# Up-projection over experts that a token block uses: count, scatter to sorted rows, gather

## The chip, the cores and the metric

One core of one Trainium2 chip. The metric is device time in microseconds of one execution, the median of several runs. TensorE (PE) multiplies matrices, VectorE (DVE), ScalarE (ACT) and GpSimd (POOL) work elementwise, and SP issues most of the DMAs.

## The reference, cut to what matters

Three transformer layers run on 256 tokens of width 1024. The last stage of the last layer is a mixture of 16,384 experts, each of which is one row of `peer_down` and one row of `peer_up`:

```python
q = (hblk @ w_q).reshape(B, TB, PEER_HEADS, 2, PEER_DHALF)
s = jnp.einsum('btphd,phnd->btphn', q, subkeys)
v, i = lax.top_k(s, PEER_TOPK)
...
tv, tj = lax.top_k(cand, PEER_TOPK)
eidx = jnp.take_along_axis(cidx, tj, axis=-1)
w = jax.nn.softmax(tv, axis=-1)
u = w_down[eidx]
a = jax.nn.gelu(jnp.einsum('btd,btpkd->btpk', hblk, u))
vv = w_up[eidx]
return jnp.einsum('btpk,btpkd->btd', (w * a), vv)
```

Each token picks 16 experts in each of 8 heads, 128 in all, by the sum of two key scores: expert = 128 x first key + second key. The result is scaled by `ga2`, added to the residual and normalised.

## The kernel before, in words

The kernel does not gather. It computes the down product of all 16,384 experts with all 256 tokens, multiplies it by a gate that is zero where a token has not picked an expert, and multiplies the result with all of the up matrix. An expert block `e` is 256 experts, two tiles `a` of 128; there are `NE` = 64 blocks. Tokens lie in two blocks `tt` of 128. Every fp32 operand is split in a high and a low part (`put_hl`, line 363; `load`, line 298: ScalarE casts `wh`, VectorE subtracts `wl`), and `mm3` (line 358) makes three matmuls of each product.

In the **gate stage** (`with tc.tile_pool(name="rp")`, lines 1457 to 1640) scores and top-16 give each token's picks. `gen_chunk` (line 1574) makes one-hot matrices `L` (first key) and `R` (second key) for 8 tokens at a time and, for each token, three matmuls `Lw x R` (line 1593): a 128 x 128 gate matrix a token. Sixteen chunks of 16 tokens go to the DRAM tensor `Gd` (line 1597). The same stage fills TensorE's gaps with the down products of the first `NST` = 28 blocks (`fill`, line 1437, with a number of steps written out by hand). TensorE runs in program order; the other engines' order is fixed by hand only while `dve.on` is set.

Then two more down blocks follow (`more_down`, line 1449: 48 matmuls in a bank `mt` and a gelu into a block `A`, one of 24 buffers and six spare ones), and then the **up stage** (lines 1655 to 1677), a loop over all 64 blocks. Every fourth block loads `G`, the gates of eight tiles (line 1659, three buffers). From block 29 on each step first does one more down block. Then the gated product is made in `pt` (line 1666), split in `ph` and `pl`, 1 MB of `up` is loaded and split, and `up` (line 1651) adds to the four accumulators `upb`, one for each token block and half of the 1024 columns. A step has 2 x 2 x 2 x 3 = 24 matmuls of 512 columns:

```python
    for e in range(NE):
        if e % 4 == 0:
            ...
        if nxt[0] < NE and nxt[0] <= e + 1:
            more_down()
        ...
        u = load(I["up"][e], 2048, 1024)
```

The last block's 24 matmuls are held back and done accumulator by accumulator beside the final normalisation (lines 1679 to 1699). Weight loads go through four 1 MB buffers `wr`, and their split parts through four `wh` and four `wl` of 1024 columns. SP issues the loads in program order; a load whose buffer is still in use holds those behind it.

Of the kernel before, what the change touches and what calls it, by code (L numbers as in the profile page):

```python
# [7 lines left out]

F32 = mybir.dt.float32
F32R = mybir.dt.float32r  # L10
BF = mybir.dt.bfloat16
U32 = mybir.dt.uint32
AF = mybir.ActivationFunctionType
ALU = mybir.AluOpType
AX = mybir.AxisListType
# [2 lines left out]

NEG = -1e30
TAIL = 8  # L20
ROOT2 = 4.0 ** 0.25
D = 1024
DFF = 2816
# [115 lines left out]
def prep(z):  # L139
    o = {}  # L140
# [65 lines left out]
    o["up"] = np.ascontiguousarray(z["peer_up_2"][0].reshape(64, 2, 128, 1024).transpose(0, 2, 1, 3).reshape(64, 128, 2048))  # L206

    vec = np.zeros((128, NVEC), np.float32)

# [38 lines left out]
def build(tc, nc, I, out, dbg=None):  # L248
# [15 lines left out]
    def acc():  # L264
        return ps.tile([P, 512], F32, tag="acc", name=nm("acc"))
# [86 lines left out]
    def mm(o, l, r, start, stop):  # L352
        pe.matmul(o, l, r, start=start, stop=stop)
# [1045 lines left out]

    pp = es.enter_context(tc.tile_pool(name="pp", bufs=1))  # L1400
    NE, NA = 64, 24
    store = {}
    nxt = [0]
    spare = []
# [52 lines left out]
    with tc.tile_pool(name="rp", bufs=1) as rp:  # L1457
# [116 lines left out]
        def gen_chunk(ch):  # L1574
            stg = rp.tile([P, P, 16], F32, tag="stg", name=nm("stg"), bufs=2)
            for q8 in range(2):
                t = (ch % 8) * 16 + q8 * 8
                L = L2[:, q8]
                R = rp.tile([P, 8, P], BF, tag="R", name=nm("R"), bufs=2)
                for i, o in ((0, L), (1, R)):  # L1580
                    dve.tensor_tensor(o.rearrange("p t (n d) -> p t n d", d=4),
                                      iota1.rearrange("p (n d) -> p n d", d=4)[:, None].to_broadcast([P, 8, 32, 4]),
                                      slotb[:, i, t:t + 8][:, :, None, :].to_broadcast([P, 8, 32, 4]), op=ALU.is_equal)
                for q4 in range(2):
                    q = slice(4 * q4, 4 * q4 + 4)
                    Lw = rp.tile([P, 4, 3, P], BF, tag="Lw", name=nm("Lw"), bufs=2)
                    dve.tensor_mul(Lw.rearrange("p t j (n d) -> p t j n d", d=4),
                                   L[:, q].rearrange("p t (n d) -> p t n d", d=4)[:, :, None].to_broadcast([P, 4, 3, 32, 4]),
                                   slotp[:, t + 4 * q4:t + 4 * q4 + 4][:, :, :, None, :].to_broadcast([P, 4, 3, 32, 4]))
                    m = mt()  # L1590
                    for i in range(4):
                        for j in range(3):
                            mm(m[:, tsl(i)], R[:, 4 * q4 + i], Lw[:, i, j], start=j == 0, stop=j == 2)
                    o = 8 * q8 + 4 * q4
# [25 lines left out]
        for tt in range(2):  # L1620
            if tt == 0:
                top16(pair_rows(0, 7))
            else:
                for h in range(0, 8, 2):
                    top16(pair_rows(1, h, 2))
                    fill(10, dve, 1)
                spare.extend(xp.tile([P, 2, 512], F32, tag="row", name="Arow", bufs=2)[:, i] for i in range(2))
# [5 lines left out]
            slots_T(tt, ev)  # L1633
            fill(10, dve, 1)
# [7 lines left out]
    dve.on = False  # L1642
    for _ in range(2):
        more_down()
    mp_ = es.enter_context(tc.tile_pool(name="mp", bufs=2))

    upb = [[acc(), acc()], [acc(), acc()]]
    G = None
    gfin = row("gfin")

    def up(e, ph, pl, u, a, tt, half):
        mm3(upb[tt][half], ph[:, a, tsl(tt)], pl[:, a, tsl(tt)], u[a][0][:, csl(half)], u[a][1][:, csl(half)],
            e == 0 and a == 0, e == NE - 1 and a == 1)

    for e in range(NE):
        if e % 4 == 0:
            G = mp_.tile([P, 16, 8, 16], F32, tag="sg", name=nm("G"), bufs=3)
            c0 = 16 if e else 14
            nc.sync.dma_start(G[:, :c0], Gd[:c0, :, 2 * e:2 * e + 8, :].rearrange("c p e t -> p c e t"))
        if nxt[0] < NE and nxt[0] <= e + 1:  # L1660
            more_down()
        A = store.pop(e)
        pt = mp_.tile([P, 2, 256], F32, tag="pt", name=nm("pt"))
        for a in range(2):
            for c in ((slice(0, 16),) if e >= 4 else (slice(0, 14), slice(14, 16))):
                dve.tensor_mul(pt[:, a].rearrange("p (c t) -> p c t", c=16)[:, c],
                               A[:, a * 256:(a + 1) * 256].rearrange("p (c t) -> p c t", c=16)[:, c],
                               Gl[:, :, (2 * e + a) % 8] if c.start else G[:, c, (2 * e + a) % 8])
        ph = mp_.tile([P, 2, 256], F32R, tag="ph", name=nm("ph"))
        pl = mp_.tile([P, 2, 256], F32R, tag="pl", name=nm("pl"))  # L1670
        put_hl(ph, pl, pt)
        u = load(I["up"][e], 2048, 1024)
        if e < NE - 1:
            for a in range(2):
                for tt in range(2):
                    for half in range(2):
                        up(e, ph, pl, u, a, tt, half)

    act_set(3)
    xf, xg = new_x(), new_x()  # L1680
    for tt in range(2):
        for half in range(2):
            for a in range(2):
                up(e, ph, pl, u, a, tt, half)
# [30 lines left out]
```

## Time and profile before

| | us |
|---|---|
| median of 3 runs | 1740.83 |
| lowest to highest | 1740.42 to 1741.88 |
| the profiled execution | 1742.32 |
| its span in the trace | 1740.5 |
| TensorE busy | 1682.9 |
| VectorE busy | 1192.7 |
| ScalarE busy | 871.5 |
| GpSimd busy | 96.9 |

Times in a trace start at 0 with its span. Matmuls are pipelined and their ends are modelled, so the distance from start to start tells more than the duration shown. "DMA share" is the mean busy share of the core's 16 DMA engines. A row `out<-in` names the tile written and those read; the line shown for most instructions is that of a helper (337), so tiles tell them apart. The gate stage runs from some 990 to 1165 us, the up stage from 1177 us to the end.

### The profile page before, as it was taken

The numbers are of one execution on the slowest core, as the hardware profiler recorded it, in microseconds if no ns is written. First come the engines' busy times: TensorE is split into PE (matmuls) and PEld (weight loads), VectorE is DVE, ScalarE is ACT, GpSimd is POOL, SyncE is SP. The second block draws the span as 40 slices with busy tenths as digits, with TensorE's granted clock in tenths as the row PEclk, the third lists the DMA queues.
The fourth block names the chain that finished last, engine by engine and source line by source line (L and its number), as shares of the span: only waits on it lengthen the run. The fifth ranks groups of instructions, "written<-read, shape, count | busy, mean of one in ns | idle before, by whom it ended". The sixth has DMA issues, their size and how long they took to land.

```text
span 1740.5 us, 28199 instructions
## 1 busy us (share of the span) xinstructions
PE 1682.9 (97%) x11374; PEld 1503.1 (86%) x11374; DVE 1192.7 (69%) x2111; ACT 871.5 (50%) x1324; POOL 96.9 (6%) x74
## 2 busy tenths in 40 slices
PE   8999999999999999889999999999999999999998
PEld 7879998788889987677789999897888999999996
DVE  5659775566688755657669999986666555555555
ACT  7545444365554444654554555554444444444444
POOL 0001000100010001111037000000000000000000
PEclk9999999999999999999999999999999999999999
DMA  8427775453468764462344465577676556656551
GB/s 315 159 73 275 272 294 187 159 205 102 157 222 319 276 218 155 173 239 98 116 167 160 162 244 210 198 269 262 236 254 217 203 209 218 208 205 215 192 177 68
DMA packets 83954, 352.01 MB, mean 202 GB/s; under 512 B 6352, under 2 KB 39504, under 8 KB 46704
## 3 DMA queue, kind: packets, MB, share of 16 engines
q1 hardware_dynamic: 83024, 349.62, 56.7%
q8 instruction: 89, 1.46, 0.3%
q10 hardware_dynamic: 288, 0.52, 0.1%
q14 instruction: 41, 0.34, 0.1%
q0 software_dynamic: 512, 0.07, 0.0%
HBM read 332.30 MB, written 17.83 MB: 201 GB/s over the span
## 4 chain that ended last, share of the span: by engine, by line
PE 87%; DVE 7%; ACT 3%; DMA 1%; issue 1%; POOL 1%; SPq 0%; DVEq 0%; ACTq 0%
PE acc L337 70%; PE mt L337 17%; DVE wl L337 2%; DVE x L337 2%; ACT wh L337 1%; ACT L337 0%; POOL x L337 0%; DMA G<-Gd 0%; DVE Lw L337 0%; DVE st L337 0%; ACT P L337 0%; DMA Gd<-stg 0%; ACT x L337 0%; DMA row<-rows 0%; DMA xt<-x_T 0%
## 5 line engine op out<-in xcount | busy, mean ns | idle before, releaser
L337 DVE TENSOR_TENSOR wl<-wr,wh 128x1024 fp32r<-128x1024 f32 (+2 forms) x504 | 606.6, 1209 | 357.2 <-ACT wh L337 355.6
L337 ACT CAST wh<-wr 128x1024 fp32r<-128x1024 f32 (+3 forms) x524 | 540.5, 1034 | 551.9 <-PE acc L337 372.8
L337 PE MATMUL acc<-xh,wh 128*128 128x256 f32 x1472 | 421.7, 286 | 0.5 <-ACT xh L337 0.5
L337 PE MATMUL acc<-xl,wh 128*128 128x256 f32 x1472 | 414.1, 281 | 0.1
L337 PE MATMUL acc<-xh,wl 128*128 128x256 f32 x1472 | 414.1, 281 | 0.0
L337 PEld LDWEIGHTS acc<-xh,wh 128*128 128x128 f32 x1472 | 278.6, 189 | 2.3 <-issue 1.2
L337 PEld LDWEIGHTS acc<-xl,wh 128*128 128x128 f32 x1472 | 279.0, 190 | 0.3 <-DVE xl L337 0.3
L337 PEld LDWEIGHTS acc<-xh,wl 128*128 128x128 f32 x1472 | 278.3, 189 | 0.0
L337 PE MATMUL acc<-wh,pl 128*128 128x512 f32 x512 | 204.9, 400 | 0.5 <-DVE pl L337 0.5
L337 PE MATMUL acc<-wh,ph 128*128 128x512 f32 x512 | 201.6, 394 | 2.0 <-ACT ph L337 2.0
L337 PE MATMUL acc<-wl,ph 128*128 128x512 f32 x512 | 202.0, 395 | 0.0
L337 PE MATMUL mt<-xh,wl 128*128 128x256 f32 x576 | 161.9, 281 | 0.0
L337 PE MATMUL mt<-xl,wh 128*128 128x256 f32 x576 | 161.8, 281 | 0.0
L337 PE MATMUL mt<-xh,wh 128*128 128x256 f32 x576 | 161.8, 281 | 0.0
L337 PE MATMUL acc<-wh,xh 128*128 128x512 f32 (+5 forms) x368 | 143.7, 390 | 15.2 <-ACT wh L337 7.2
L337 PE MATMUL acc<-wh,xl 128*128 128x512 f32 (+5 forms) x368 | 140.2, 381 | 3.3 <-DVE xl L337 3.3
L337 PE MATMUL acc<-wl,xh 128*128 128x512 f32 (+5 forms) x368 | 140.5, 382 | 1.2 <-DVE wl L337 1.2
L337 PEld LDWEIGHTS acc<-wl,ph 128*128 128x128 f32 x512 | 96.6, 189 | 23.6
L337 PEld LDWEIGHTS acc<-wh,ph 128*128 128x128 f32 x512 | 96.7, 189 | 23.4 <-ACT ph L337 2.2
L337 PEld LDWEIGHTS acc<-wh,pl 128*128 128x128 f32 x512 | 96.5, 188 | 23.2 <-DVE pl L337 1.0
L337 PEld LDWEIGHTS mt<-xl,wh 128*128 128x128 f32 x576 | 108.6, 189 | 1.4
L337 PEld LDWEIGHTS mt<-xh,wh 128*128 128x128 f32 x576 | 108.5, 188 | 1.5
(290 smaller groups left out, 2252.6 us busy)
## 6 DMA issues: line engine op xcount, KB each, us to landing
wr<-f SPq DMA_DIRECT2D x64, 1024.0 KB, 5.8
wr<-dn SPq DMA_DIRECT2D x64, 1024.0 KB, 4.9
wr<-up SPq DMA_DIRECT2D x64, 1024.0 KB, 5.0
wr<-ada SPq DMA_DIRECT2D x24, 1024.0 KB, 6.6
Gd<-stg SPq DMA_DIRECT2D x16, 1024.0 KB, 4.7
G<-Gd SPq DMA_DIRECT2D x15, 1024.0 KB, 7.8
wr<-m_g SPq DMA_DIRECT2D x10, 1024.0 KB, 5.0
row<-rows SPq DMA_DIRECT2D x16, 512.0 KB, 4.5
```

The source lines that it names most:

```text
L337: inst = f(*args, **kw)
```

## The change

The up matrix is given as plain rows (`up` of 16384 x 1024) instead of packed blocks. The first 16 blocks (`NS`, 32 tiles, 4096 experts) stay as they are and are called static. For the other `NJ` = 96 tiles:

1. `gen_chunk` adds one matmul a token, `R x L` without a weight, into one accumulator bank held for the whole stage: how often each of the 12,288 experts is picked, for each token block.
2. Between two down blocks the counts become four classes (block 0 only, both, block 1 only, none), and small matmuls with a triangular matrix give each expert a position `posi` in that order. A flag is set if a class boundary breaks the constants `T0`, `T1`, `T2`.
3. All remaining down blocks are done before the first gathered row is used. `weigh` multiplies a block by its gates: static blocks in place, the others into `pt`, with the expert's own index beside the product, and GpSimd scatters 128 rows of 264 numbers to the DRAM tensor `Pd` at `posi`. One static up block comes before every fourth down block, nine in all.
4. After three more static up blocks, `row_up` reads sorted tiles of `Pd`, GpSimd gathers the 128 rows of `up` whose indices lie in them, and only those (tile, token block) pairs are multiplied that the constants allow. Fully used pairs of tiles and half-used ones alternate.
5. Behind them, every engine reads the flag, and a conditional block would do all other pairs. Then the last static block and the normalisation follow; `gfin` is loaded there.

```diff
+NS = 16
+NJ = 128 - 2 * NS
+T0, T1, T2 = 61, 20, 83
...
+                        mm(cnt_b[0][:, ch // 8 * NJ:(ch // 8 + 1) * NJ], R[:, 4 * q4 + i], L[:, 4 * q4 + i, 2 * NS:],
+                           start=n == 0, stop=n == 127)
...
-    for _ in range(2):
+    more_down()
...
+    W = 264
+    Pd = nc.dram_tensor("Pd", (NJ * P, W), F32, kind="Internal").ap()
+    Pv = dram_disjoint_views(Pd, NJ)
...
+    for c in range(4):
+        mm(b[:NJ, tsl(c)], M[:, c], oneb, start=c == 0, stop=c == 3)
+    act.copy(wk[:NJ, 192:448].bitcast(BF), b[:NJ])
+    more_down()
+    b = mt()
+    mm(b[:, :4 * NJ], tri, wk[:, 0:192].bitcast(BF), start=True, stop=False)
+    for c in range(4):
+        o = b[:, c * NJ:(c + 1) * NJ]
+        mm(o, totb[:, c], tri[:NJ, :NJ], start=False, stop=False)
+        for c_ in range(c):
+            mm(o, totb[:, c_], oneb[:NJ, :NJ], start=False, stop=False)
+        mm(b[:, 4 * NJ + c:4 * NJ + c + 1], totb[:, c], oneb[:NJ, 0:1], start=False, stop=c == 3)
...
+    for i, (n, op) in enumerate(((T1, ALU.is_lt), (T0, ALU.is_gt), (T2, ALU.is_gt))):
+        dve.tensor_scalar(few[:, i:i + 1], few[:, i:i + 1], 128.0 * n, None, op0=op)
...
+                G = mp_.tile([P, 16, 8, 16], F32, tag="sg", name=nm("G"), bufs=2)
...
+    def weigh(e):
+
+        G, A = gates(e), store[e]
+        if e < NS:
+            for a in range(2):
+                for c in ((slice(0, 16),) if e >= 4 else (slice(0, 14), slice(14, 16))):
+                    o = A[:, a * 256:(a + 1) * 256].rearrange("p (c t) -> p c t", c=16)[:, c]
+                    dve.tensor_mul(o, o, Gl[:, :, (2 * e + a) % 8] if c.start else G[:, c, (2 * e + a) % 8])
+            return
+        pt = mp_.tile([P, 2, W + 8], F32, tag="pt", name=nm("pt"), bufs=5)
+        for a in range(2):
+            i = 2 * e + a
+            pool_.iota(pt[:, a, 128:136].bitcast(I32), pattern=[[0, 8]], base=i * P, channel_multiplier=1)
...
+        for a in range(2):
+            j = 2 * (e - NS) + a
+            nc.gpsimd.indirect_dma_start(Pv[j], bass.IndirectOffsetOnAxis(ap=posi[:, j:j + 1], axis=0), pt[:, a, 0:W], None)
+        store.pop(e)
...
+    def row_parts(i, used):
+
+        tts = set(used[0]) | set(used[1])
+        tiles = [a for a in range(2) if used[a]]
+        o, n = (0, W) if len(tts) == 2 else (128 * min(tts), 136)
+        Pc = mp_.tile([P, 2, W + 8], F32, tag="pt", name=nm("Pc"), bufs=5)
...
+        for a in tiles:
+            nc.gpsimd.indirect_dma_start(r[:, a * 1024:(a + 1) * 1024], None, I["up"],
+                                         bass.IndirectOffsetOnAxis(ap=Pc[:, a, 128:129].bitcast(U32), axis=0))
...
+    for g in (0, 4, 5, 6, 1, 7, 8, 2, 9, 3, 10, 11, 12, 13, 14, 15):
+        work.extend(range(4 * g, 4 * g + 4))
...
+    su = 0
+    weigh_some(5)
+    while nxt[0] < NE:
+        if (nxt[0] - 30) % 4 == 0:
+            static_up(su)
+            su += 1
         more_down()
...
+        weigh_some(2)
+    nxt[0] += 1
+    weigh_some(len(work))
+
+    def blocks_of(j):
+        return [tt for tt, t in ((0, j < T0), (1, T1 <= j < T2)) if t]
...
+    lead = 3
+    for _ in range(lead):
+        static_up(rest.pop(0))
+    gap = len(seq) // (len(rest) + 1)
+    for n, q in enumerate(seq):
+        row_up(*q)
+        if rest and n % gap == gap - 1:
+            static_up(rest.pop(0))
...
+    v = nc.values_load(flag[0:1, 0:1])
...
+    with tc.If(v > 0, preferred_fallthrough_block=False):
...
+        for i, used in out_of:
+            ph_, pl_, u_ = row_parts(i, used)
...
     gfin = row("gfin")
```

## Rows read from the trace of the kernel before

**Rows 1.** The page: busy time by engine; GpSimd in the 40 slices.

```profile
PE 1682.9 (97%) x11374; PEld 1503.1 (86%) x11374; DVE 1192.7 (69%) x2111; ACT 871.5 (50%) x1324; POOL 96.9 (6%) x74
...
POOL 0001000100010001111037000000000000000000
```

**Rows 2.** Windows: stretch, length, busy (count) of the engines, PEclk, DMA share, GB/s.

```profile
1200.00:1300.00 100.00, 100.00 (x431) 80.42 (x430) 68.03 (x89) 46.94 (x54) 0.00 (x0) 1.00 0.69 240
1600.00:1700.00 100.00, 100.00 (x643) 90.55 (x642) 54.49 (x61) 46.29 (x54) 0.00 (x0) 1.00 0.53 189
```

**Rows 3.** Chain of waits: start, us, engine, tile, count; one pattern to 1720 us.

```profile
1348.06 5.59 PE acc L337 x24
1353.65 5.70 PE mt L337 x48
```

**Rows 4.** Windows as in rows 2, of two more stretches.

```profile
1342.00:1478.00 136.00, 136.00 (x869) 122.94 (x868) 74.09 (x84) 62.60 (x73) 0.00 (x0) 1.00 0.61 212
510.00:520.00 10.00, 10.00 (x87) 10.00 (x86) 8.77 (x11) 5.24 (x9) 0.00 (x0) 1.00 0.98 360
```

**Rows 5.** Groups of 1180 to 1718 us: count, busy us, mean ns, idle.

```profile
L337 DVE TENSOR_TENSOR wl<-wr,wh 128x1024 fp32r<-128x1024 f32 x190 | 232.8, 1225 | 197.0 <-ACT wh L337 197.0
L337 ACT CAST wh<-wr 128x1024 fp32r<-128x1024 f32 x191 | 200.6, 1050 | 248.3 <-PE acc L337 127.3 <-PE mt L337 116.1 <-issue 5.0
...
L337 DVE TENSOR_TENSOR pl<-pt,ph 128x512 fp32r<-128x512 f32 x61 | 42.0, 689 | 26.9 <-ACT ph L337 26.9
L337 DVE TENSOR_TENSOR pt<-A,G 128x256 f32<-128x256 f32 x106 | 41.8, 420 | 0.7
...
L337 ACT ACTIVATE A<-mt 128x512 f32<-128x512 f32 x33 | 19.6, 594 | 0.0
```

**Rows 6.** Groups of GpSimd, whole span, columns as in rows 5.

```profile
L337 POOL DMA_DIRECT2D qk<-dqk x16 | 8.4, 531 | 102.5 <-PE mt L337 53.7 <-DVE dqk L337 48.8
...
L288 POOL MEMSET epsln<- 128x1 f32 x1 | 0.1, 98 | 0.3 <-POOLq L1708 0.3
```

**Rows 7.** Timeline of TensorE in the gate stage: start, us, what, count.

```profile
1010.07 0.84 PE L337 MATMUL mt<-Lw,R 128*128 128x128 bf16 x12
1010.72 0.36 PE L337 MATMUL acc<-xh,wh 128*128 128x256 f32 x1
```

**Rows 8.** Waits of TensorE, 1000 to 1163.7 us: total, times, longest.

```profile
PE mt L337 <- DVE Lw L337: 4.0, 5, 2.2
```

**Rows 9.** Timeline of TensorE at the start of the up stage.

```profile
1177.40 0.50 PE L337 MATMUL acc<-wh,ph 128*128 128x512 f32 x1 [2.02 <-ACT ph L337]
...
1180.13 0.63 PE L337 MATMUL acc<-wh,pl 128*128 128x512 f32 x1
1180.55 0.63 PE L337 MATMUL acc<-wh,ph 128*128 128x512 f32 x1
```

**Rows 10.** Timeline of VectorE there: half a block's products (four in a row).

```profile
1179.14 0.39 DVE L337 TENSOR_TENSOR pt<-A,G 128x224 f32<-128x224 f32 x1
1179.45 0.19 DVE L337 TENSOR_TENSOR pt<-A,Gl 128x32 f32<-128x32 f32 x1
```

**Rows 11.** GpSimd's DMAs of 4 KB by tile: min/median/max ns; landing in us.

```profile
L337 POOL DMA_DIRECT2D qk<-dqk x16: 518/518/702, 388.5 to 450.1; - x16
...
DMA to landing us min/median/max: 1.6/3.7/6.0
```

**Rows 12.** DMA queues and issues: count, KB each, median us to landing.

```profile
q0 software_dynamic: 512, 0.07, 0.0%
...
row<-rows SPq DMA_DIRECT2D x16, 512.0 KB, 4.5
...
cw<-cw2v SPq DMA_DIRECT2D x1, 64.0 KB, 3.2
```

**Rows 13.** The up loads by tile: landing in us.

```profile
DMA to landing us min/median/max: 4.8/5.0/10.3
```

**Rows 14.** Waits of SP's queue: a meeting of engines at the kernel's start.

```profile
SPq L1708 <- PEq L1708: 0.7, 1, 0.7
```

More of the change, by code (lines that the diff above doesn't have):

```diff
@@ L1626, in build @@
                     fill(10, dve, 1)
-                spare.extend(xp.tile([P, 2, 512], F32, tag="row", name="Arow", bufs=2)[:, i] for i in range(2))
+                Ar = xp.tile([P, 2, 512], F32, tag="row", name="Arow", bufs=2)
+                spare.extend(Ar[:, i] for i in range(2))
             ev = slots(tt)
@@ new lines, in build, with __call__ @@
+    dve.tensor_add(few[:, 0:1], few[:, 0:1], few[:, 1:2])
+    flag = few[:, 4:5].bitcast(I32)
+    dve.tensor_add(flag, few[:, 0:1], few[:, 2:3])
+    upb = [[acc(), acc()], [acc(), acc()]]
+    class Gates:
+        tiles = {}
+        def __call__(self, e):
+            g = e // 4
+            if g not in self.tiles:
+                G = mp_.tile([P, 16, 8, 16], F32, tag="sg", name=nm("G"), bufs=2)
+                c0 = 16 if g else 14
+                nc.sync.dma_start(G[:, :c0], Gd[:c0, :, 8 * g:8 * g + 8, :].rearrange("c p e t -> p c e t"))
+                self.tiles[g] = G
+            return self.tiles[g]
@@ new lines, in hl_pair, with parts, up @@
+    def hl_pair():
+        return (mp_.tile([P, 2, 256], F32R, tag="ph", name=nm("ph")),
+                mp_.tile([P, 2, 256], F32R, tag="pl", name=nm("pl")))
+    def parts(r, used=(0, 1)):
+        ws = {}
+        for a in used:
+            h = wp.tile([P, 1024], F32R, tag="wh", name=nm("wh"), bufs=4)
+            l = wp.tile([P, 1024], F32R, tag="wl", name=nm("wl"), bufs=4)
+            put_hl(h, l, r[:, a * 1024:(a + 1) * 1024])
+            ws[a] = (h, l)
+        return ws
+    def up(banks, ph, pl, u, a, tt, half, first, last):
+        mm3(banks[tt][half], ph[:, a, tsl(tt)], pl[:, a, tsl(tt)], u[a][0][:, csl(half)], u[a][1][:, csl(half)],
+            first, last)
@@ new lines, in static_parts, with static_up @@
+    def static_parts(e):
+        ph, pl = hl_pair()
+        put_hl(ph, pl, store.pop(e).rearrange("p (a t) -> p a t", a=2))
+        r = wp.tile([P, 2048], F32, tag="wr", name=nm("wr"), bufs=4)
+        nc.sync.dma_start(r.rearrange("p (a d) -> p a d", a=2),
+                          I["up"][2 * e * P:(2 * e + 2) * P].rearrange("(a p) d -> p a d", a=2))
+        return ph, pl, parts(r)
+    def static_up(e):
+        ph, pl, u = static_parts(e)
+        for a in range(2):
+            for tt in range(2):
+                for half in range(2):
+                    up(upb, ph, pl, u, a, tt, half, e == 0 and a == 0, False)
@@ new lines, in row_up, with weigh_some @@
+    def row_up(i, used):
+        ph, pl, u = row_parts(i, used)
+        for a in range(2):
+            for tt in used[a]:
+                for half in range(2):
+                    up(upb, ph, pl, u, a, tt, half, False, False)
+    work = []
+    for g in (0, 4, 5, 6, 1, 7, 8, 2, 9, 3, 10, 11, 12, 13, 14, 15):
+        work.extend(range(4 * g, 4 * g + 4))
+    def weigh_some(n):
+        while work and n and work[0] < max(nxt[0] - 1, NS):
+            weigh(work.pop(0))
+            n -= 1
@@ new lines, in build @@
+    su = 0
[4 more added lines that the diff above has]
+            su += 1
+        more_down()
+        weigh_some(2)
[3 more added lines that the diff above has]
+        return [tt for tt, t in ((0, j < T0), (1, T1 <= j < T2)) if t]
+    order_ = [(i, (blocks_of(2 * i), blocks_of(2 * i + 1))) for i in range(NJ // 2)]
+    two = [x for x in order_ if len(x[1][0]) + len(x[1][1]) == 4]
+    one = [x for x in order_ if 0 < len(x[1][0]) + len(x[1][1]) < 4]
@@ new lines, in build @@
+    one = [x for xs in zip(one[:len(one) // 2], one[len(one) // 2:]) for x in xs] + one[2 * (len(one) // 2):]
+    seq = []
+    while two or one:
+        if two:
+            seq.append(two.pop(0))
+        if one:
+            seq.append(one.pop(0))
+    rest = list(range(su, NS - 1))
+    lead = 3
[6 more added lines that the diff above has]
+            static_up(rest.pop(0))
@@ new lines, in build @@
+    while rest:
+        static_up(rest.pop(0))
+    e = NS - 1
+    ph, pl, u = static_parts(e)
+    v = nc.values_load(flag[0:1, 0:1])
+    engines = (pe, dve, act, pool_)
+    for eng in engines:
+        eng.last = None
+    with tc.If(v > 0, preferred_fallthrough_block=False):
+        more = [[mt(), mt()], [mt(), mt()]]
+        out_of = [(i, [[tt for tt in range(2) if tt not in blocks_of(2 * i + a)] for a in range(2)]) for i in range(NJ // 2)]
+        out_of = [(i, used) for i, used in out_of if used[0] or used[1]]
+        todo = [[(i, a) for i, used in out_of for a in range(2) if tt in used[a]] for tt in range(2)]
+        for i, used in out_of:
+            ph_, pl_, u_ = row_parts(i, used)
+            for a in range(2):
+                for tt in used[a]:
+                    for half in range(2):
+                        up(more, ph_, pl_, u_, a, tt, half, (i, a) == todo[tt][0], (i, a) == todo[tt][-1])
+        for tt in range(2):
+            for half in range(2):
+                t = block()
+                dve.tensor_mul(t, more[tt][half], ga[:, 1, csl(half)])
+                dve.tensor_add(x[:, tt, csl(half)], x[:, tt, csl(half)], t)
@@ L1679, in build @@
+    for eng in engines:
+        eng.last = None
+    gfin = row("gfin")
     act_set(3)
```

79 lines of the change are left out of this document (47 added, 32 removed).

## The prediction

> **What bounds the kernel now.** I read the views from the whole to the part. The page first: TensorE is busy for 1682.9 of 1740.5 us, VectorE 69%, ScalarE 50%, GpSimd 6%, and GpSimd does nothing after slice 22 of 40 [rows 1]. The windows then show where TensorE has slack: in two stretches of 100 us between 1200 and 1700 us it has none, at the full granted clock, and VectorE falls from 68 to 54 us busy [rows 2]. The chain of waits gives the unit of this stage: 48 down matmuls of one expert block in 5.70 us and 24 up matmuls in 5.59 us, one directly behind the other [rows 3]. So from some 1180 us on the time is a count of matmuls; whatever takes matmuls away there pays in full as long as nobody makes TensorE wait. Last I read what could do that: the DMA engines [rows 4], VectorE and ScalarE [rows 5], GpSimd [rows 6].
>
> **What is removed.** One pair of an expert tile and a token block is 6 of those 24 matmuls, 5.59/4 = 1.40 us [rows 3]. Before there are 128 tiles x 2 blocks = 256 pairs. After, the 32 static tiles keep 64; of the 96 sorted tiles block 0 takes 61 and block 1 takes 83 - 20 = 63. That leaves 188, so 68 pairs go: 68 x 1.40 = **-95.0 us**. The bounds 61, 20 and 83 are constants; if the counts break them, the conditional block does the rest. Counting from the reference's routing on its default inputs, of the 12,288 sorted experts 2720 serve block 0 alone, 4866 both, 2775 block 1 alone: 2720 is above 20 x 128 = 2560, 7586 below 7808, 10361 below 10624. The block is then skipped.
>
> **Counting.** 256 matmuls of 96 columns join the gate stage. There 12 matmuls of 128 columns take 1010.07 to 1010.72, 0.054 us each [rows 7]: 13.8 us, or 10.4 if a column fewer is a column cheaper. TensorE is nearly full in this stretch too; it waits 4.0 us for Lw [rows 8], which the new work can fill. Bounds 6 and 14, taken **+10**. One accumulator bank of four is held meanwhile; the blocks being filled use one at a time.
>
> **Ranks and flag.** Four matmuls of 128 columns, one of 384 and 14 small ones, at 0.054 us per 128 columns: **+1**. The VectorE steps between them lie under the two down blocks placed around them.
>
> **Start of the stage.** Before, TensorE stands idle for 2.0 us here until G is weighed, and then runs slower for a while: matmuls start 0.42 us apart [rows 9] where 5.59/24 = 0.23 is normal. After, five blocks are weighed ahead of the first static block's conversion instead of one. A block costs four products, 2 x (0.39 + 0.19) = 1.16 us [rows 10], so about 4.3 us more VectorE work is ahead of it, less 1 us of rank matmuls: **+3**. Bounds: -4 (the old stall gone) and +6.
>
> **Down stage, 34 blocks and 9 static ups** (with the first two blocks and three leading static ups 272 us of TensorE). Per block VectorE has two conversions at 1.23, up to four products at 0.42 and a quarter of a static block (3.1/4), 4.9 us; ScalarE 3.4; a block with its share of static ups lasts 5.70 + 1.40 = 7.1 [rows 3, 5]. Both are covered. If that cover goes, TensorE waits for wl. The DMA engines are closer. A 1 MB load costs 2.94 us of all 16 engines (1600 to 1700: 53% of 100 us for 18.0 loads [rows 2]); a G load, in 512-byte pieces, 3.6 us (1342 to 1478: 83 us for 27.5 MiB [rows 4], three of them G loads, since one comes with every four pairs of 11.29 us). So 28 ns for 512 bytes and 368 ns for 8 KB on an engine. A straight line gives a 1056-byte row 52 ns, a scatter of 128 rows 0.42 us; its bounds are 0.22 and 2.94. Demand: 36 down loads 106, 12 up loads 35, 16 G loads 58, 96 scatters 40 = 239 of 272 us. But two blocks are weighed per down block until they catch up, so in the first 24 down blocks it is 166 of 170 us. The engines have been at 98% with TensorE full [rows 4], so I take **+3** for late loads; bounds 0 and +30. The G loads stand in SP's queue before later weight loads and now have two buffers instead of three: a late product holds G, and SP behind it.
>
> **GpSimd** gets 96 index fills, 96 scatters and 83 gathers. The trace has no indirect DMA. The nearest row is a GpSimd DMA of 4 KB, 0.53 us to issue on average [rows 6], 0.52 in the median and 0.70 at worst [rows 11], with 512/16 = 32 packets each [rows 12]. With 128 packets it is 0.52 if the issue is a fixed cost and 2.07 if it goes by packets; I take 1.3, halfway, since the row is far from both. Fills: 0.1 each, by the memsets [rows 6]. Then the first 24 down blocks need 74 x 1.4 = 104 of 170 us, and the row stage 83 x 1.3 = 108 of 196: nothing on the path. The VectorE products wait for one of five pt buffers, so a slow GpSimd would reach TensorE through VectorE's queue.
>
> **From scatter to gather.** No row can be read before the last scatter has landed. After the last down block: gelu 0.59, two products 0.84, two scatters 2.6, landing 3.7 [rows 11], a read of Pd 3.2 as the nearest small load [rows 12], gather issue 1.3, landing 5.0 [rows 13], conversion 1.05 + 1.23 [rows 5] = 19.5 us. Three static ups cover 3 x 5.59 = 16.8. **+3** with some clock lost; bounds 0 and 11 (landings of 6.0 and 10.3 [rows 11, 13]).
>
> **Row stage**, 124 x 1.40 + 4 x 5.59 = 196 us: gathers of 128 rows of 4 KB at 187 ns, 1.49 us each, 124; Pd reads at most 35; four up loads 12: 171 us of DMA. VectorE needs 3.1 us for a full pair of tiles and 2.9 for a half-used one, against 5.6 and 2.8 of TensorE, which alternate: covered. **0**.
>
> **The condition.** All engines read the flag and branch before the last block. No row shows a branch. The ends are two meetings of engines as at the kernel's start (0.7 us [rows 14]), 1.4, and two meetings with two instruction loads at 5 us and the lower clock, 13. I take one load at 3.2 us, the landing of a small load [rows 12], and the meetings: **+5**. The gfin row is now loaded after it: landing 4.5 us [rows 12] against the 5.59 us of the last 24 matmuls: hidden, mostly.
>
> **Sum:** -95 + 10 + 1 + 3 + 3 + 3 + 5 = -70 us. The span is 1740.5, the profiled execution 1742.32, the median of the runs 1740.83, 1.5 us below it. Forecast 1740.8 - 70 = **1671 us**; with all terms at their ends except the DMA's, 1651 to 1694.
>
> **Rivals.**
> (a) *The DMA engines become the bound.* For it: 166 of 170 us. Against it: 98% was reached without harm. If a scatter costs 0.84, the first 24 blocks need 197 us: +27, with other terms the same about 1695 to 1712, say **1698**. Chance 0.15.
> (b) *GpSimd waits for VectorE at each indirect DMA.* VectorE subtracts for 1.23 us at a time with both inputs in SBUF [rows 5]. If each indirect DMA waits for one of them, its price is 1.3 + 1.23 = 2.53: the row stage then needs 210 us of 196, and the first 24 blocks up to 195 of 170; -70 + 14 to 39 gives 1685 to 1710, **1700**. Chance 0.10. By the Trainium skill, "SBUF — State Buffer", section "Who interferes with whom", an instruction of VectorE with two SBUF inputs contends with a GpSimd instruction that reads SBUF, as one reading its indices does. No run so far shows it.
> (c) *GpSimd becomes the bound and the kernel slower.* It does 179 indirect DMAs beside 272 + 196 = 468 us of TensorE work; with 10 us of fills, the gain is gone when 179p + 10 = 468 + 70, at p = 2.95 us. The slowest row times four is 2.81 [rows 11], just short of it, and gives 1716. At 3.3 us it is **1804**. Chance 0.07.
> (d) *The change does not do what it says:* the counts break a bound and the conditional block runs. It does the 68 pairs after all, 95 us, behind a fresh start of 19 us: **1785**. The counts above speak against it. Chance 0.02.
> The forecast gets 0.62; 0.04 is left for sums of ends near no change.
>
> **Numbers.** The range 1650 to 1712 takes the forecast's own 1651 to 1694 and most of (a) and (b). About 0.2%, 3.5 us, is what a measurement of this kernel can tell from no change. Faster: 0.62 + 0.15 + 0.10 and a little of the rest, 0.88; same 0.03; slower 0.07 + 0.02, 0.09.
>
> **What would show it.** Right: the chain of waits is TensorE up to the end, up matmuls down from 1536 to 1128, GpSimd issues near 1.3 us with idle time between them, one gap of a few us before the first gathered rows and one before the last 24 matmuls. Wrong: TensorE waiting in many small pieces for wh, wl or ph (then DMA share near 1 points to (a), GpSimd without idle to (b) or (c)); a second long run of gathers after the flag (d); a gate stage longer by more than 14 us.

## The result, and the profile after

| | before | after |
|---|---|---|
| median of the runs made together, us | 1741.28 | 1686.2 |
| ratio, with its 95% interval | | 0.9678, 0.9659 to 0.9697 |
| the profiled execution, us | 1742.32 | 1687.74 |
| its span, us | 1740.5 | 1685.9 |

The forecast was 1671 us in a range of 1650 to 1712. The time is in the range, and 15 us above the forecast. Single executions of the changed kernel and of several kernels below were disturbed and took 1 to 4% longer; the ratios leave these out, so a ratio, or the span of the profiled execution, is what counts below.

The page of the changed kernel, busy time by engine, then GpSimd and the granted clock in the 40 slices [rows 1]:

```profile
PE 1608.8 (95%) x11241; PEld 1445.0 (86%) x11241; DVE 1167.7 (69%) x2110; ACT 851.5 (51%) x1307; POOL 324.0 (19%) x350
...
POOL 0001000001010000110104600000573333554550
PEclk9999999999999999999999999999889999999998
```

TensorE's busy time fell by 74 us and the span by 55. Its share fell from 97 to 95%, and the granted clock, at 9 in all 40 slices before, is at 8 in the last slice and in slices 29 and 30: 1180 to 1264 us, the beginning of the down stage. The windows there [rows 2] (stretch, length, busy time and count of each engine, PEclk, DMA share, GB/s):

```profile
1200.00:1220.00 20.00, 15.75 (x128) 15.31 (x126) 8.12 (x17) 7.81 (x9) 14.79 (x23) 0.97 0.77 251
1220.00:1240.00 20.00, 17.47 (x106) 16.19 (x107) 13.79 (x26) 6.77 (x8) 13.24 (x22) 0.86 0.93 315
1240.00:1260.00 20.00, 14.03 (x97) 13.75 (x96) 12.38 (x22) 4.77 (x6) 16.80 (x20) 0.83 0.79 263
1260.00:1280.00 20.00, 20.00 (x148) 18.92 (x148) 12.49 (x22) 9.28 (x11) 7.45 (x12) 1.00 0.95 336
1280.00:1300.00 20.00, 20.00 (x164) 19.74 (x163) 12.14 (x16) 9.29 (x11) 7.13 (x9) 1.00 1.00 348
...
1600.00:1660.00 60.00, 60.00 (x258) 48.28 (x257) 40.19 (x42) 35.31 (x43) 26.52 (x23) 1.00 0.77 263
```

From 1200 to 1260 us TensorE is idle for 12.8 us and its granted clock is 0.83 to 0.97. From 1260 us on it is full, although the DMA engines are at 95 and 100% there, more than in the stretches with stalls. The row stage (last line) is full too. So by far the largest loss has one place. What the engines wait for between 1195 and 1457 us (waiting engine and tile, what it waits for, total us, times, longest), first TensorE, then VectorE, then GpSimd:

```profile
PE mt L342 <- DVE wl L342: 12.7, 3, 6.0
...
DVE pt L342 <- DMA Pd<-pt,wk: 21.3, 6, 7.0
...
POOL pt L342 <- DMA Pd<-pt,wk: 104.8, 30, 6.0
```

TensorE waits for the low part of a down matrix, VectorE for a pt buffer whose scatter has not landed, and GpSimd, in 30 index fills, for the same. The groups of GpSimd from 1180 to 1457 us, columns as in [rows 6], then the gathers of 1460 to 1670 us:

```profile
L1741 POOL DMA_INDIRECT Pd<-pt,wk x92 | 116.5, 1266 | 45.0 <-issue 16.5 <-POOL pt L342 14.3 <-DVE wk L342 11.4
L342 POOL IOTA pt<- 128x8 int32 x96 | 10.0, 138 | 110.6 <-DMA Pd<-pt,wk 104.8 <-DMA Gd<-stg 5.7
...
L1787 POOL DMA_INDIRECT wr<-up,Pc x83 | 95.9, 1155 | 89.3 <-DVE wl L342 59.2 <-issue 17.4 <-DMA Pc<-Pd 6.4
```

Put together by stage, each stage's length taken between TensorE's own matmuls (down blocks at 5.70 us and up blocks at 5.59 [rows 3] are the undisturbed length):

| step | forecast, us | measured, us |
|---|---|---|
| 68 pairs away | -95.0 | -95 (94.3 in a run below) |
| up to the first gate matmul | 0 | +3.5 |
| counting, in the gate stage | +10 | +9.4 |
| rank matmuls | +1 | +0.8 |
| start of the stage | +3 | +2 |
| down stage | +3 | +17.7 |
| scatter to gather | +3 | +2.2 |
| row stage | 0 | 0 |
| condition and tail | +5 | +5.2 |
| sum | -70 | -54 |

The spans differ by 54.6 us. The 3.5 us lie ahead of everything that the change touches, and are a difference between two executions: in the eleven kernels below, whose code is the same up to there, the first gate matmul starts anywhere from 989.8 to 999.2 us. That is why stages, and not spans, are compared.

The 17.7 us are in the eight down blocks behind the first two static ups: four of them take 30.6 and four 32.7 us instead of 22.8, so there are two stalls, of 7.8 and 9.9 us. All later ones take 22.8. The same code loses 15.9 us there in the run without the condition and 18.0 us in the run with all pairs: between two executions, some 2 us of this stage are chance.

The first stall, line by line (GpSimd's first scatter, then VectorE):

```profile
1193.62 4.89 POOL L1741 DMA_INDIRECT Pd<-pt,wk  x1 [11.40 <-DVE wk L342]
...
1218.89 0.76 DVE L342 TENSOR_TENSOR pt<-A,G 128x256 f32<-128x256 f32 x2 [7.01 <-DMA Pd<-pt,wk]
```

From 1193.62 to 1217.16 us GpSimd does 14 scatters with no more than 0.31 us between them: here it is not idle, it is behind. VectorE waits 7.01 us for a buffer that one of them still holds, and the `wl` that TensorE needs stands behind that wait.

### The profile page after: what moved, and what is told of

It is laid out like the page before. It is cut to its first block, busy times and chain, and to the rows that moved or that the text cites. A ratio compares the mean times of both kernels' runs of the same rounds, so it can differ in the third digit from the quotient of the medians.

```text
span 1685.9 us, 28633 instructions
## 1 busy us (share of the span) xinstructions
PE 1608.8 (95%) x11241; PEld 1445.0 (86%) x11241; DVE 1167.7 (69%) x2110; ACT 851.5 (51%) x1307; POOL 324.0 (19%) x350
## 5 line engine op out<-in xcount | busy, mean ns | idle before, releaser
L342 DVE TENSOR_TENSOR wl<-wr,wh 128x1024 fp32r<-128x1024 f32 (+2 forms) x491 | 589.1, 1207 | 289.7 <-ACT wh L342 288.4
L342 ACT CAST wh<-wr 128x1024 fp32r<-128x1024 f32 (+2 forms) x511 | 526.7, 1034 | 491.8 <-PE acc L342 297.3
L342 PE MATMUL acc<-wh,xh 128*128 128x512 f32 (+5 forms) x368 | 146.0, 397 | 15.9 <-ACT wh L342 7.6
L342 PE MATMUL acc<-wh,pl 128*128 128x512 f32 x376 | 149.8, 398 | 2.5 <-DVE pl L342 2.5
L342 PE MATMUL acc<-wh,ph 128*128 128x512 f32 x376 | 149.6, 398 | 1.9 <-ACT ph L342 1.3
L342 PE MATMUL acc<-wl,ph 128*128 128x512 f32 x376 | 149.5, 398 | 0.8 <-DVE wl L342 0.8
L342 POOL TENSOR_TENSOR x<-x,row 128x256 f32<-128x256 f32 x16 | 23.5, 1468 | 566.1 <-ACT x L342 565.4
L1741 POOL DMA_INDIRECT Pd<-pt,wk x96 | 121.0, 1261 | 46.2 <-issue 17.7
L342 PEld LDWEIGHTS mt<-xh,wl 128*128 128x128 f32 x576 | 110.8, 192 | 13.4 <-DVE wl L342 13.4
L1787 POOL DMA_INDIRECT wr<-up,Pc x83 | 95.9, 1155 | 89.3 <-DVE wl L342 59.2
```

Source lines behind the costliest of these rows:

```text
L342: inst = f(*args, **kw)
L1741: nc.gpsimd.indirect_dma_start(Pv[j], bass.IndirectOffsetOnAxis(ap=posi[:, j:j + 1], axis=0), pt[:, a, 0:W], None)
L1787: nc.gpsimd.indirect_dma_start(r[:, a * 1024:(a + 1) * 1024], None, I["up"], bass.IndirectOffsetOnAxis(ap=Pc[:, a, 128:129].bitcast(U32), ...
```

## The experiments

**The condition.** The edit:

```diff
-    v = nc.values_load(flag[0:1, 0:1])
...
-    with tc.If(v > 0, preferred_fallthrough_block=False):
...
```

> The reading of the flag and the conditional block are left out, the rest stays. Theory: the condition is what makes the tail behind the last matmul 5.2 us longer than before (13.8 against 8.6 us), so the time falls by about 5 us, to 1681 us from some 1686, and the tail is about 8.6 us again. Rival: the tail is longer because the final sums lost their old overlap with the last matmuls; then the time falls by 1 us or less.

Ratio 0.9633 (0.9611 to 0.9655), span 1676.5. The last matmul's line (start, us):

```profile
1667.09 0.40 PE L342 MATMUL acc<-wh,pl 128*128 128x512 f32 x1
```

The tail behind it is 1676.5 - 1667.5 = 9.0 us. With the condition it is 1685.9 - 1672.1 = 13.8, by these lines of the changed kernel (the last matmul, the first VectorE instruction behind the condition, and the load of a function table on ScalarE):

```profile
1671.67 0.40 PE L342 MATMUL acc<-wh,pl 128*128 128x512 f32 x1
...
1674.44 1.89 DVE L342 TENSOR_TENSOR x<-x,x 128x512 f32<-128x512 f32 x3 [3.06 <-issue]
...
1677.42 1.28 ACT L342 ACT_TABLE_LOAD   x1
```

In the tail the condition costs 4.8 us, as the theory had it: VectorE stands for 3.06 us with nothing to wait for, and the sums and the square roots that used to run beside the last matmuls come behind them. The ratios differ by more, 7.8 us; the rest lies ahead of the tail, where the code is the same and executions differ by chance.

VectorE's reading of the flag (ns, and when), the loads of instructions that the DMA engines do from 1671.6 to 1674.4 us, in the gap, and the same VectorE instruction in the kernel with both orders (below):

```profile
L1850 DVEq TENSOR_LOAD <-wk x1: 545/545/545, 1670.7 to 1670.7; - x1
...
q8 instruction: 1, 0.02, 3.3%
q14 instruction: 1, 0.01, 1.2%
...
1654.23 1.90 DVE L342 TENSOR_TENSOR x<-x,x 128x512 f32<-128x512 f32 x3 [0.69 <-DVEq L1880]
```

The flag is read in 0.55 us under the last multiplication, and the branch is over at 1671.59 us; 2.86 us of the gap lie behind it. Nine kernels have the condition at this place. Four of them (the changed kernel, and those with nearly nothing counted, with GpSimd's order and with half of the G loads) go on 2.8 to 2.9 us after the branch, with two such loads in between, and have tails of 13.7 to 14.2 us. In the other five VectorE goes on 0.5 us after the branch, with no load in between, and the tails are 11.4 to 11.9 us. So the condition costs 4.8 us in the changed kernel, and only 2.4 to 2.9 more than the 9.0 us without it where no load has to be waited for. The Trainium skill, "Runtime: NRT & Kernel Launch", section "Instruction fetch mechanics", says that a taken branch whose target is not yet at hand waits for a fetch of instructions. The gap and the loads in it agree with that; for which engine a load is, the trace doesn't tell.

**Counting.**

```diff
+                        if n in (0, 127):
                             mm(cnt_b[0][:, ch // 8 * NJ:(ch // 8 + 1) * NJ], ...
...
-    for i, (n, op) in enumerate(((T1, ALU.is_lt), (T0, ALU.is_gt), (T2, ALU.is_gt))):
+    for i, (n, op) in enumerate(((-1, ALU.is_lt), (200, ALU.is_gt), (200, ALU.is_gt))):
```

> Only the first and the last token of each block are counted (4 counting matmuls instead of 256), and the flag's bounds are widened so that the conditional block is not entered; the sorted places then no longer follow the real use. Theory: TensorE is full in the gate stage, so the 252 matmuls are the 12.9 us that this stage grew by: the time falls by about 13 us, to 1673. Rival: the bank held for the counts (it is still held here), or VectorE's pace, is what lengthens the stage: the time falls by less than 4 us.

Ratio 0.9658 (0.9606 to 0.971), span 1681.1: only 4.8 us less, and by spans the case would be open. The stage itself settles it. TensorE's first gate matmul and first matmul of the next down block, for the kernel before, the changed kernel and this one, in turn:

```profile
990.59 1.26 PE L337 MATMUL mt<-Lw,R 128*128 128x128 bf16 x12 [3.29 <-DVE Lw L337]
...
1163.83 0.28 PE L337 MATMUL mt<-xh,wh 128*128 128x256 f32 x1
```

```profile
994.11 0.48 PE L342 MATMUL mt<-Lw,R 128*128 128x128 bf16 x3 [3.28 <-DVE Lw L342]
...
1176.74 0.28 PE L342 MATMUL mt<-xh,wh 128*128 128x256 f32 x1
```

```profile
999.20 0.33 PE L342 MATMUL mt<-Lw,R 128*128 128x128 bf16 x3 [3.29 <-DVE Lw L342]
...
1173.02 0.28 PE L342 MATMUL mt<-xh,wh 128*128 128x256 f32 x1
```

The stage takes 173.2 us before, 182.6 with counting, and 173.8 with the bank held but nearly nothing counted. In the ten other kernels of this study, all with counting, it takes 182.9 to 183.9. So counting costs 9 to 10 us, and the held bank less than 1. Half of it did not show in the span, because this execution came to the stage 5.1 us later than the changed kernel's. The expectation's 12.9 us held the 3.5 us ahead of the stage, so its theory is right and its size is not.

**All pairs.**

```diff
-T0, T1, T2 = 61, 20, 83
+T0, T1, T2 = NJ, 0, NJ
...
-    with tc.If(v > 0, preferred_fallthrough_block=False):
...
```

> The bounds are set so that all 96 sorted tiles serve both token blocks (256 pairs instead of 188, 96 gathers instead of 83); the conditional block, which has nothing to do then, and the reading of the flag are left out. Against the run without the condition (about 1677 us). Theory: TensorE is the limit of the row stage, and each pair costs 6 matmuls, 1.40 us: 68 pairs add 95 us, 1770 to 1774. Rival: the row stage has a floor of its own from gathers and reads, so that the pairs taken away did not pay in full; then less than 90 us are added.

Ratio 1.0185 (1.0162 to 1.0207), span 1774.4. The part of TensorE's work behind the last down block grows from 912 matmuls in 215.05 us (the run without the condition) to 1320 in 309.36: 94.3 us for 68 pairs, 1.39 us each. The windows of this run in the row stage:

```profile
1500.00:1700.00 200.00, 200.00 (x858) 160.98 (x857) 112.01 (x108) 94.41 (x108) 90.52 (x66) 1.00 0.76 234
```

TensorE is full with all pairs, as it is with fewer in the changed kernel. The gain was paid in full, and it was not in this stage that part of it was lost.

**VectorE's order.** VectorE's queue holds products and conversions, in an order that the build's planner chooses unless `dve.on` is set. Two kernels set it from the first static up to the last down block, one with the code's order, one with the next job's conversions ahead of the products:

```diff
     weigh_some(5)
+    dve.on = True
     while nxt[0] < NE:
...
+    dve.on = False
```

> In the down stage VectorE is bound to the order in which the code stands: the products of two blocks, then the conversions of the next job. Theory A (the products of up to five blocks, each waiting for a pt buffer, stand ahead of the conversions in VectorE's queue; the lost 17.7 us of the first eight blocks are this order): with only two blocks ahead of any conversion the loss falls to about half, 1674 to 1680 us. Rival B (loads are late, because the DMA engines are nearly full): unchanged, 1683 to 1687.

```diff
     while ready:
         (kind, e), w = ready.pop(0)
...
+        if jobs:
+            convert(jobs.pop(0))
         if kind == "d":
             weigh_some(2)
```

> As the run with the order of the code, but the conversions of the next job stand ahead of the two blocks' products. Theory A: TensorE has a whole job in hand while VectorE waits for a pt buffer, so of the 17.7 us at most 4 are left: 1668 to 1673 us, with no wait of mt for wl over 2 us. Rival B (late loads): unchanged, 1683 to 1687. Rival C (GpSimd cannot keep up with two blocks per job): part is won, but waits of some us each come back through the whole first 24 blocks, 1676 to 1683.

Both were slower than the changed kernel: ratio 0.9765 (0.9745 to 0.9784) for the code's order, 0.9722 (0.9697 to 0.9748) for the other. None of the theories had that. With the code's order the down stage loses 35.5 us. In the second one the waits between 1195 and 1457 us, of TensorE, VectorE and GpSimd, are:

```profile
PE mt L342 <- DVE wl L342: 12.2, 3, 5.4
PE acc L342 <- DVE wl L342: 9.6, 2, 7.0
...
DVE pt L342 <- DMA Pd<-pt,wk: 64.4, 17, 8.2
...
POOL pt L342 <- DMA Pd<-pt,wk: 121.3, 38, 7.3
```

Behind the first static up the blocks ran without a gap, but stalls came at 1279 us and from 1352 us on, 32.5 us in the down stage in all. VectorE waits three times as long for landed scatters as in the changed kernel. Something other than VectorE's order made buffers come back late. GpSimd's timeline at the second stall of the changed kernel shows it (start, us; the fills `IOTA` are two to a block, the scatters `DMA_INDIRECT` too):

```profile
1233.63 1.49 POOL L1741 DMA_INDIRECT Pd<-pt,wk  x1 [0.30 <-issue]
1235.13 0.40 POOL L342 IOTA pt<- 128x8 int32 x4
1236.79 0.21 POOL L342 IOTA pt<- 128x8 int32 x2 [1.25 <-DMA Pd<-pt,wk]
1240.01 0.21 POOL L342 IOTA pt<- 128x8 int32 x2 [3.01 <-DMA Pd<-pt,wk]
1240.77 1.74 POOL L1741 DMA_INDIRECT Pd<-pt,wk  x1 [0.54 <-DVE pt L342]
1242.81 0.96 POOL L1741 DMA_INDIRECT Pd<-pt,wk  x1 [0.30 <-issue]
```

and VectorE's beside it:

```profile
1232.06 1.09 DVE L342 TENSOR_TENSOR pt<-A,G 128x256 f32<-128x256 f32 x3 [3.50 <-DMA G<-Gd]
...
1248.79 0.80 DVE L342 TENSOR_TENSOR pt<-A,G 128x256 f32<-128x256 f32 x2 [6.81 <-DMA Pd<-pt,wk]
1249.52 1.21 DVE L342 TENSOR_TENSOR wl<-wr,wh 128x1024 fp32r<-128x1024 f32 x1
```

The eight fills are those of four later blocks, and they stand in GpSimd's queue ahead of a block whose two products were made by 1233 us. GpSimd is free at 1235.13, but that block's scatters start at 1240.77, 5.6 us later, when the last of the fills has got its buffer. (The product named at 1240.77 is one of a later block that happened to end just then.) Their landing lets VectorE go on at 1248.79, after a wait of 6.81 us, and only behind those products comes the `wl` that TensorE waits for. In the run with conversions first the same lag is longer: the products of the eighth scattered block end at 1219.94 us and its scatters start at 1239.92. This became theory D: fills of later blocks hold up scatters that are ready, so buffers come back late, and products that wait for them hold up conversions.

**GpSimd's order, and both orders.** The scatters go through the wrapper that keeps the code's order: fills of a block, its scatters, the next block.

```diff
     su = 0
+    pool_.on = True
...
-            nc.gpsimd.indirect_dma_start(Pv[j], ...
+            pool_.indirect_dma_start(Pv[j], ...
```

> GpSimd is bound to the order in which the code stands: the index fills of one block, then its two scatters, then the next block. VectorE's order is left as it was but for single instructions. Theory D, formed from the trace of the changed kernel (index fills of up to four later blocks, each waiting for a pt buffer, stand in GpSimd's queue ahead of scatters whose products are ready, so that a landing of some 6 us is paid again and again): GpSimd's waits of a fill for a landed scatter, 27.4 us in 8 waits between 1180 and 1300 us, fall below 10, and of the 17.7 us that the down stage loses some 8 to 14 come back: 1672 to 1678 us from some 1685. Rival A (VectorE's own order alone, products ahead of the conversions): little changes, 1681 to 1686. Rival B (loads late): unchanged, 1683 to 1687.

> Both orders: GpSimd as the code stands, and VectorE bound to the conversions of the next job ahead of the products of two blocks. With VectorE bound alone the time was about 1692 us, with 123 us of GpSimd waiting in 39 fills for a landed scatter and TensorE stalled late in the stage. Theory D: those waits go, and with a whole job in hand TensorE does not wait in the down stage: 1666 to 1672 us. Rival A' (the pt buffers are too few in any order, five of them for a landing of 6 to 9 us): 1680 us or more, with stalls of some us left beyond 1260 us. Rival B (loads late): 1683 or more.

GpSimd's order alone: ratio 0.9661 (0.9641 to 0.9681), about 1682 us. Its interval overlaps the changed kernel's, so by the ratio no gain is certain. In the profiled execution the down stage loses 11.1 us instead of 17.7, less was won than theory D wanted. The first stall is still there, 7.6 us against 7.8; the second one shrank from 9.9 to 3.5. Both orders: ratio 0.9573 (0.9559 to 0.9587), median 1667.64 us, and the down stage loses nothing. Waits of VectorE and TensorE in the first, between 1195 and 1457 us:

```profile
PE mt L342 <- DVE wl L342: 7.9, 3, 5.2
...
DVE pt L342 <- DMA Pd<-pt,wk: 13.7, 4, 5.2
DVE A L342 <- DMA G<-Gd: 10.1, 2, 8.9
```

With both orders, TensorE's only wait from 1180 to 1457 us and GpSimd's longest one:

```profile
PE acc L342 <- DVE wl L342: 4.5, 1, 4.5
...
POOL Pd L342 <- DVE pt L342: 112.1, 22, 14.8
```

and a window of 100 us of that kernel:

```profile
1200.00:1300.00 100.00, 100.00 (x769) 96.44 (x768) 63.82 (x95) 45.88 (x54) 50.20 (x80) 1.00 0.91 313
```

In both kernels no fill waits for a scatter any more. With both orders GpSimd waits for products: its scatters start at most 3.2 us after the products of their block. With its order alone they still lag by up to 9.3 us in the first eighteen blocks, since products come faster than it scatters them. In the changed kernel they lag by up to 27 us, but there the largest lags come late in the stage, when only one block is weighed per down block, and stall nobody. With GpSimd's order alone, VectorE still had products ahead of conversions, and waited there for a late G (10.1 us) and for buffers (13.7 us). The four cases of the down stage's loss, from one profiled execution each:

| | VectorE as planned | VectorE: conversions first |
|---|---|---|
| GpSimd as planned | 17.7 us | 32.5 us |
| GpSimd in the code's order | 11.1 us | 0 us |

So neither queue's order alone is the cause; the loss goes when both are bound. Conversions first also means that each block's load is asked for one job earlier; no run parts the two, but by itself that order didn't help. Late loads are not the cause: with both orders the DMA engines are at 91% from 1200 to 1300 us, more than the changed kernel's 89%; scatters take 6.2 us to land in the median, against 5.0; and TensorE is full.

**Half of the G loads.**

```diff
-            g = e // 4
+            g = e // 4 if e < 8 else e // 4 // 2 * 2
```

> From the third group on, two groups of blocks use the gates of one load: 9 G loads instead of 16, 14 MB less; the products are made with the wrong gates for half of these groups. Rival B (the DMA engines, at 77 to 100% of their time between 1180 and 1300 us, make loads and landings late): of the 17.7 us lost in the down stage most come back, 1670 to 1676 us. Theory D (the order of GpSimd's queue, with landings that take 6 us from other reasons): 1681 to 1686 us.

The profiled execution took 1680.4 us, between the two forecasts, and its down stage loses 13.8 us; only one other execution was undisturbed (1676.6), so there is no ratio. With seven loads of 1 MB gone (not the 14 MB of the expectation) that is 2 to 4 us less than in the three executions that lose 15.9 to 18.0 us. The rest stayed at a DMA share of 79% from 1200 to 1300 us. Traffic may make the wait a little longer; it doesn't make it.

**The start of the stage.** What was left with both orders is the first static up. One more down block goes ahead of it, and VectorE weighs and converts static block 0 before the rank sums and the other four blocks:

```diff
-    weigh_some(5)
...
+    jobs = [("d", 30), ("s", 0)]
...
+    convert(jobs.pop(0))
+    weigh_some(1)
+    convert(jobs.pop(0))
+    ranks()
...
+        if e == 30 and kind == "d":
+            weigh_some(4)
+            continue
```

> Both orders as in the run before (1667.6 us), and the stage's start is turned round: one more down block stands ahead of the first static up, and VectorE weighs and converts static block 0 ahead of the rank sums and of the other four blocks. Theory: the 6.7 us that the first static up still loses there is the wait for G's landing and the weighing of five blocks, which the 5.70 us of a down block cover: 1661 to 1664 us. Rival: the stall only moves (GpSimd's first scatter, held up by later rank sums, makes VectorE late for the next blocks): 1666 to 1669.

Ratio 0.9529 (0.9516 to 0.9542), median 1658.8 us, 9 us less than with both orders, a little more than was hoped. A window of 100 us:

```profile
1200.00:1300.00 100.00, 100.00 (x784) 96.71 (x783) 66.47 (x101) 45.97 (x53) 54.47 (x86) 1.00 0.94 329
```

and TensorE's only wait from 1195 to 1457 us:

```profile
PE acc L342 <- DVE wl L342: 0.8, 1, 0.8
```

From the first extra down block to the last, TensorE now takes 254.4 us, as 36 down and nine up blocks should (255.5). Some 2 us of the gain are down blocks of 5.63 us instead of 5.70, for a reason that is open. The two halves of this edit were not run apart.

**A sixth buffer.**

```diff
-        pt = mp_.tile([P, 2, W + 8], F32, tag="pt", name=nm("pt"), bufs=5)
+        pt = mp_.tile([P, 2, W + 8], F32, tag="pt", name=nm("pt"), bufs=6)
```

> As the run with the start turned round, with six pt buffers instead of five (the two small constant tiles go to a tile that is free at that time). Theory D (order, not the number of buffers, was the limit): within 2 us of that run. Rival A' (too few buffers): 2 to 6 us faster than that run.

Ratio 0.952 (0.9507 to 0.9533), median 1657.64: within the other's interval, as theory D had it. Five buffers are enough with these orders; whether a sixth would have helped the changed kernel was not run.

**The condition further ahead.** The same block of lines, moved ahead of `static_parts` of the last expert block.

> As the run with the start turned round, with the condition ahead of the last expert block's conversions instead of behind them, so that its cost stands within the row of matmuls and not in the tail. Theory (the cost is mostly VectorE's and ScalarE's restart in the tail, 4.8 us, while TensorE has matmuls left): 1 to 4 us are won against that run. Rival (every engine stands still for the condition wherever it is, TensorE too, and its clock falls after it): the same time, or up to 5 us more.

Ratio 0.9537 (0.952 to 0.9553), median 1660.58: not faster. The rival's time holds, its reason only in part. The tail shrinks from 11.9 to 9.4 us, but TensorE's matmuls behind the last down block take 221.2 instead of 214.2 us:

```profile
1636.77 0.40 PE L342 MATMUL acc<-wh,pl 128*128 128x512 f32 x1
1640.99 0.80 PE L342 MATMUL acc<-wh,ph 128*128 128x512 f32 x1 [3.83 <-ACT wh L342]
1641.58 0.63 PE L342 MATMUL acc<-wl,ph 128*128 128x512 f32 x1
```

The chain of waits has what TensorE stood for:

```profile
1632.86 5.42 DMA wr<-up
```

The edit also puts the last block's load behind the condition: it is issued at 1632.86 us, where the kernel with the start turned round issues it at 1624.30. It lands after 5.42 us, two conversions follow, and TensorE has stood for 3.83 us. Then it starts matmuls 0.42 us apart instead of 0.23, at a granted clock of 0.50 from 1640 to 1645 us, the lower of its two levels (1.2 GHz); twelve of them cost 2.3 us more. Of the two places tried, the end was the better one; the condition ahead of the conversions but behind that load was not run.

## Why the prediction was right, and where it was off

**The count of matmuls** was right: 68 pairs at 1.40 us, measured 94.3 us for the reverse step. That the row stage pays in full was right too, with gathers at 1.16 us and 0.30 between them.

**Counting** at +10 was right, +9.4. **Ranks** at +1 were 0.8. **The start** at +3 was about +2: the first static up waited 1.34 us for `ph` and 2.53 us for `pl`, behind the rank sums and four blocks that were not yet needed.

**The down stage is the term that was mis-sized:** +3 for late loads, and 17.7 us measured. The text had the path in a sentence, that a slow GpSimd would reach TensorE through VectorE's queue and the pt buffers. It dropped it, because GpSimd's work fitted: 104 of 170 us. GpSimd's price of 1.3, a middle between two far bounds, came near the mean by luck: a scatter holds it for 1.26 us on average, 0.97 where VectorE does nothing beside it, and the next one starts 0.30 later. What failed is the step from "it has time" to "nothing on the path": in the first stall GpSimd had a backlog while it fitted on average, in the second it was idle in front of ready work. The scatter's landing was not part of the sum, and the question of what stands behind each fill and each product in an in-order queue was not asked. Nor did the text ask who sets that order: it says in the description of the kernel that all but TensorE run in the planner's order unless bound. The 30 us at the far end of that term's bounds held the loss, though by another cause.

**Scatter to gather** at +3 was +2.2. **The condition** at +5 was +5.2, of which taking it away gives back 4.8. That gfin's load would be hidden was right, but not in the way forecast: it was issued at 1258 us, in the down stage, and not after the condition.

**The rivals.** (a) The DMA engines as the bound: they reach 100% in the slice from 1280 to 1300 us without a stall, and the run with both orders, at 91%, speaks against it. (b) GpSimd waiting for VectorE at each indirect DMA, 2.53 us each: not at each and not at that price, but the wait is there. Of the 96 scatters of the changed kernel 19 ran with no VectorE instruction beside them, and took 0.96 to 0.98 us; the other 77 took 1.33 on average and up to 6.18. One of these, and the VectorE instruction beside it:

```profile
1313.78 2.02 POOL L1741 DMA_INDIRECT Pd<-pt,wk  x1 [0.53 <-POOL pt L342]
...
1313.72 1.23 DVE L342 TENSOR_TENSOR wl<-wr,wh 128x1024 fp32r<-128x1024 f32 x1 [0.96 <-ACT wh L342]
```

It ends 0.85 us after that subtraction does. Over the changed kernel and the eleven others, 603 of the 612 indirect DMAs that took more than 1.2 us end 0.78 to 0.90 us after a VectorE instruction, the other nine 0.95 us after one. So the first scatter's 4.89 us are a wait too: VectorE works without a gap from 1192.73 to 1197.56 us. Some 5.7 us of GpSimd's backlog in the first stall come from such waits; no run takes them away, so their share in the 7.8 us is open. By themselves they don't make the loss: with both orders scatters still take up to 4.27 us, and TensorE is full. By the Trainium skill, "SBUF — State Buffer", section "Who interferes with whom", a VectorE instruction with two SBUF inputs contends with a GpSimd instruction that reads SBUF. The trace agrees with that, by the 2.02 us above against 0.96; in this stage VectorE hardly does anything else than such instructions, so others aren't compared. (c) needed 2.95 us for each indirect DMA; 1.26 and 0.30 are far from it. (d) The block behind the flag did not run: 83 gathers, no more.

Of what would show the forecast wrong, one sign was there: TensorE waiting in pieces for `wl`. The text had tied that to the DMA share or to a GpSimd without idle time. In the first stall GpSimd was indeed without idle time, as (b) and (c) had it. In the second it was idle, and that was the clue: it was idle in front of work that was ready.

## What to carry to other kernels

An engine with time to spare can still be the cause of a stall: look at what stands behind a waiting instruction in its queue, and whether that was ready. When a producer and a consumer share a ring of buffers, an instruction that only claims a buffer should stand directly ahead of the work that will free it, and conversions for the engine that sets the pace ahead of everything that can wait. Here the orders of two queues that feed each other had to be changed together: one alone won little, the other alone lost. Stages of single executions are compared by their own first and last instruction.

## What the runs showed of the hardware

- An indirect scatter of 128 rows of 1056 bytes holds GpSimd for 0.96 to 0.99 us when VectorE does nothing beside it (192 scatters of twelve kernels), and the next one starts 0.30 us after its end. A gather of 128 rows of 4 KB holds it for 0.93 to 0.96 us then (143 gathers): four times the bytes for the same number of rows cost GpSimd nothing more.
- Beside VectorE's subtractions and products, from SBUF to SBUF, some of them wait until one of these, or a row of them without a gap, has ended, and end 0.78 to 0.95 us after it: 6.18 us at worst in the changed kernel, 8.73 in the one with GpSimd's order.
- Landings of scatters take 2.4 to 11.7 us. In the run with fewer G loads their median was 4.1 instead of 5.0 us, so part of it may be traffic; the rest is open.
- A condition whose block isn't entered cost 4.8 us at the end of the changed kernel, of which 2.86 are VectorE's wait behind its branch; in five other kernels that wait was 0.5 us. Within a row of matmuls it cost TensorE 7 us: 3.83 us of waiting for a load behind it, and 2.3 us at the lower clock.
- The DMA engines at 91 to 94% for 100 us, and 100% for 20, went with a TensorE that was full.
